# Stores and cache refills are issued from a lane that waits for the kernel's own count of engine time

## The chip, the cores and the metric

The kernel runs on one core of one Trainium2 chip. The metric is the device time of one execution in microseconds. A profile of one execution lists every instruction of the engines (TensorE = PE, VectorE = DVE, ScalarE = ACT, GpSimd = POOL) and the transfers that their queues issue; SyncE (SP) does nothing but issue transfers, in the order of its queue, and a transfer that must wait for its producer holds all that stands behind it.

## The reference

One layer of a hybrid encoder with D = 2048: 512 prompt tokens and 8 × 16 sample tokens, 640 columns together, float32.

```
z  = x @ w_in                     # all input projections in one
yA = (fox_attend(q, k, v, c) * silu(gate_a)) @ w_out_fox      # 8 heads of 128
       # logits + cumulative log forget gates, causal;
       # the sample tokens also see a cache of 512 keys and values per sequence
yB = (rms_norm(delta(q', k', v', g, beta)) * silu(gate_b)) @ w_out_gdn   # 8 heads of 128
       # q'|k'|v' = silu(depthwise conv of width 4); chunks of 64 tokens:
       # amat = I + strict_lower(kb @ k^T * decay)
       # u, w = triangular_solve(amat, v*beta), triangular_solve(amat, kb*exp(gc))
       # then a scan over chunks with a 128 x 128 state
h  = (sigmoid(m_a)*yA + sigmoid(m_b)*yB) @ w_out
x1 = LayerNorm(alpha*x + h)
y  = x1 + sigmoid(x1 @ w_pl_gate) * rms_norm(p @ w_pl_proj)
```

Outputs are y, the new keys, values and log forget values, the last convolution rows and the final DeltaNet states.

## The kernel before

**The stream.** Every large projection is cut into columns of 128 outputs; a column is a row of matmuls of 128x128 by 128x320 (two halves of the 640 tokens). For float32 accuracy each operand is split into a high and a low part (xh, xl, wh, wl), so that a product costs three matmuls. Some pairs of columns are done in a form with seven instead of eight block products; GpSimd forms the sums of their weights (ws, sb) ahead. Weights come by SyncE into tiles wr of 512 KB (three buffers, L269); ScalarE casts the high part (wh, L329) and VectorE subtracts it (wl, L335), or GpSimd fetches wl by a transfer that accumulates. These columns keep TensorE's queue filled.

**The steps between.** Attention and DeltaNet are Python generators, kept in lanes (`self.lane`). After every six matmuls of the stream the main program calls `tick()`. It looks at each lane in turn and, where the first generator of the lane is due, runs it to its next `yield`. `yield n` asks for n steps of pause; a negative n lets the next part start before the modelled end of the work just issued. The program is emitted under a manual schedule, so each engine's queue holds its instructions in the order in which these steps emit them.

**The planner.** While it emits, the kernel counts: `self.clock` is the modelled time of TensorE, advanced with each matmul, and `self.busy[e]` the modelled end of the last instruction of VectorE, ScalarE and GpSimd. A lane is due when its wake step and its modelled time have come.

**The stages that the change touches.** From about 730 to 960 us the stream carries the FoX heads (`phase_fox`). Per head: q, k, v are fetched from where they were stored; the bias rows nb and nbd are loaded (L637, L639); the prompt part goes through scores (L388), xs, pn; the sample part goes over the cached keys kc (`fox_dec`, scores at L773) and values vc (L813). When the scores over kc are done, the four kc loads for the next head are issued (`load_kv`, L627), and after the values the four vc loads. Each head's result og is stored to the scratch ogd (L830).

From about 960 to 1620 us the stream carries the DeltaNet heads (`phase_gdn`). A head's triangular matrix lt is inverted in blocks of 32 (`gdn_blocks`): four stores put the diagonal blocks to the scratch ld (L993), one load brings them back as lanes of 80 partitions (L998), and VectorE runs 31 pairs of a product and a subtraction on sx, which starts as the identity (L1004 and L1006). sx is stored (L1012), loaded again as u0 by `gdn_feed` (L1023), and `gdn_merge` puts the blocks of 32 together into uu: small matmuls on TensorE and copies on ScalarE and VectorE (L1060, L1068, L1072, L1074). uu is read by the head's scan over chunks (L1196, S at L1206). Beside that run the convolution of later channels (strip L865, cy L877 and L880, whose tail is stored at L884), the merge gates m (stored as md, L1572) and the FoX output projection fx (stored as fd, L1712).

The lanes are made in this order, in which each step visits them:

```
        self.outs, self.decs = self.lane(), self.lane()
        work, conv, self.ends = self.lane(), self.lane(True), self.lane()
        self.blocks, self.feeds, self.merge = self.lane(True), self.lane(True), self.lane()
        self.chunks, self.sums = self.lane(), self.lane(True)
```

## Time and profile before

| what | value |
|---|---|
| three runs | 2169.94, 2173.96, 2173.36 us; median 2173.36 |
| the profiled execution: its own time | 2173.18 us |
| its span in the profile | 2171.3 us |
| granted TensorE clock, mean | 0.999 |
| PE / DVE / ACT / POOL busy | 2149.0 / 1566.0 / 1007.3 / 401.9 us |
| bytes moved by DMA | 452.65 MB, mean 208 GB/s |

All rows come from that one execution. The page gives each engine's busy time and the groups of instructions by line; the windows give the same for a stretch of the span; the waits list says which instruction stood idle and whose end released it; the timeline lists single instructions by start, with the idle time before each in brackets. "SPq" is SyncE's queue: a wait there is time in which the transfer at its head could not be issued. Names as in `sx<-sx,lanes` are output and inputs. "L1004" is a line of the kernel before.

### The profile page before, as it was taken

The page shows a single profiled execution, that of the slowest core. Times are in us where ns is not written, and L with a number is a line of the kernel's source. Part 1 is how long each engine was busy: PE and PEld are TensorE (multiplying, and loading weights), DVE is VectorE, ACT ScalarE, POOL GpSimd, SP SyncE. Part 2 cuts the span into 40 slices and gives each one's busy share as a digit, 9 for nine tenths or more (in the row PEclk, how much of TensorE's full clock was granted, in tenths as well). Part 3 has the DMA queues.
Part 4 walks back from the last instruction along what each step waited for, and adds up shares of the span by engine and source line. Part 5 has one row for each costly group of instructions (what it writes and reads, how often), then busy time and mean ns, then how long its engine had stood idle before and what let it go on. Part 6 is the DMA issues. An engine that isn't in the chain of part 4 may idle for free.

```text
span 2171.3 us, 41951 instructions
## 1 busy us (share of the span) xinstructions
PE 2149.0 (99%) x15438; PEld 2082.3 (96%) x15438; DVE 1566.0 (72%) x3207; ACT 1007.3 (46%) x2213; POOL 401.9 (19%) x596
## 2 busy tenths in 40 slices
PE   9999999999999999999999999999999999999998
PEld 7799999999999998899999999999999999999998
DVE  5877776767776565566478677766757787789987
ACT  4344443443444343353655566655443343354544
POOL 0022233323330101002334333332000000021100
PEclk9999999999999999999999999999999999999999
DMA  6356656666554899869978778878567656673465
GB/s 235 101 184 202 189 182 199 198 199 194 184 180 158 276 325 344 314 199 291 241 179 199 180 188 194 189 182 248 161 229 260 209 171 202 201 276 122 153 227 173
DMA packets 240670, 452.65 MB, mean 208 GB/s; under 512 B 38920, under 2 KB 122504, under 8 KB 240464
## 3 DMA queue, kind: packets, MB, share of 16 engines
q1 hardware_dynamic: 224912, 421.64, 59.5%
q0 software_dynamic: 15552, 28.32, 8.0%
q8 instruction: 122, 2.00, 0.4%
q14 instruction: 84, 0.69, 0.1%
HBM read 353.48 MB, written 96.38 MB: 207 GB/s over the span
## 4 chain that ended last, share of the span: by engine, by line
PE 91%; DVE 3%; DMA 3%; ACT 1%; SPq 0%; issue 0%; POOL 0%; ACTq 0%; DVEq 0%; POOLq 0%
PE g L474 44%; PE g L396 18%; PE g L397 18%; PE g L440 2%; PE s L974 1%; PE s L742 1%; PE s L813 1%; PE s L773 1%; DMA ws138b<-ws 0%; PE s L440 0%; PE s L1168 0%; DMA nb<-rd 0%; DVE sx L1006 0%; DVE sx L1004 0%; PE s L726 0%
## 5 line engine op out<-in xcount | busy, mean ns | idle before, releaser
L329 ACT CAST wh<-wr 128x512 fp32r<-128x512 f32 x624 | 381.2, 619 | 288.7 <-PE g L474 109.5
L335 DVE TENSOR_TENSOR wl<-wr,wh 128x512 fp32r<-128x512 f32 x516 | 358.3, 708 | 183.5 <-ACT wh L329 173.7
L474 PE MATMUL g<-xh,wh 128*128 128x320 f32 (+1 forms) x1296 | 402.9, 311 | 2.7 <-ACT m L1278 1.6
L474 PE MATMUL g<-xl,wh 128*128 128x320 f32 (+1 forms) x1296 | 401.2, 310 | 0.6 <-DVE xl L371 0.6
L474 PE MATMUL g<-xh,wl 128*128 128x320 f32 (+1 forms) x1296 | 401.4, 310 | 0.0
L396 PE MATMUL g<-xh,wh 128*128 128x320 f32 (+1 forms) x960 | 313.0, 326 | 0.7 <-ACT wh L329 0.7
L396 PE MATMUL g<-xh,wl 128*128 128x320 f32 (+1 forms) x960 | 297.1, 309 | 0.8 <-DMA wl<-in_w 0.7
L396 PE MATMUL g<-xl,wh 128*128 128x320 f32 (+1 forms) x960 | 297.2, 310 | 0.4 <-DVE xl L371 0.4
L397 PE MATMUL g<-xh,wh 128*128 128x320 f32 x960 | 297.3, 310 | 0.0
L397 PE MATMUL g<-xl,wh 128*128 128x320 f32 x960 | 297.0, 309 | 0.0
L397 PE MATMUL g<-xh,wl 128*128 128x320 f32 x960 | 296.7, 309 | 0.0
L474 PEld LDWEIGHTS g<-xh,wh 128*128 128x128 f32 x1296 | 243.9, 188 | 4.3 <-ACT m L1278 2.1
L474 PEld LDWEIGHTS g<-xl,wh 128*128 128x128 f32 x1296 | 243.7, 188 | 1.1 <-DVE xl L371 1.1
L474 PEld LDWEIGHTS g<-xh,wl 128*128 128x128 f32 x1296 | 244.1, 188 | 0.0
L474 PE MATMUL g<-t,wh 128*128 128x320 f32 (+1 forms) x1088 | 241.4, 310 | 0.0
L335 DVE TENSOR_TENSOR wl<-sr,wh 128x512 fp32r<-128x512 f32 x200 | 147.9, 759 | 98.6 <-ACT wh L329 97.6
L295 POOL TENSOR_TENSOR ws<-ws 128x171 f32<-128x171 f32 (+2 forms) x152 | 116.7, 768 | 541.5 <-DMA ws<-in_w 535.7
L396 PEld LDWEIGHTS g<-xh,wh 128*128 128x128 f32 x960 | 180.9, 188 | 11.9 <-issue 7.1
L474 PEld LDWEIGHTS g<-t,wh 128*128 128x128 f32 x1088 | 181.9, 188 | 0.6 <-issue 0.3
L396 PEld LDWEIGHTS g<-xh,wl 128*128 128x128 f32 x960 | 180.6, 188 | 1.4 <-DMA wl<-in_w 1.0
L397 PEld LDWEIGHTS g<-xh,wh 128*128 128x128 f32 x960 | 181.0, 189 | 0.9
L396 PEld LDWEIGHTS g<-xl,wh 128*128 128x128 f32 x960 | 180.9, 188 | 1.0 <-DVE xl L371 1.0
(440 smaller groups left out, 4148.8 us busy)
## 6 DMA issues: line engine op xcount, KB each, us to landing
wr<-in_w SPq DMA_DIRECT2D x252, 512.0 KB
wl<-in_w POOLq DMA_DIRECT2D x108, 256.0 KB, 5.8
kc<-in_kc SPq DMA_DIRECT2D x32, 512.0 KB
vc<-in_vc SPq DMA_DIRECT2D x32, 512.0 KB
sr<-in_w SPq DMA_DIRECT2D x25, 512.0 KB
ws<-in_w SPq DMA_DIRECT2D x96, 128.0 KB
sb<-in_w SPq DMA_DIRECT2D x80, 128.0 KB
md<-m SPq DMA_DIRECT2D x32, 320.0 KB
```

The source lines that it names most:

```text
L295: nc.gpsimd.tensor_tensor(out=o, in0=x, in1=y, op=op)
L329: nc.scalar.copy(out=hi, in_=src)
L335: nc.vector.tensor_tensor(out=lo, in0=src, in1=hi.bitcast(F32), op=ALU.subtract)
L396: nc.tensor.matmul(ps[0], whl[w], xhl[o][:, a], start=(first and x == 0), stop=(last and x == 2))
L397: nc.tensor.matmul(ps[1], whl[w], xhl[o][:, b], start=(first and x == 0), stop=(last and x == 2))
L440: nc.tensor.matmul(ps, x[:, sl], w, start=(s == 0 and n == 0), stop=(s == 15 and n == 2))
L474: nc.tensor.matmul(ps, a[:, w], b, start=(k == 0 and n == 0 and not more), stop=(k == last and n == 2), skip_group_check=True)
L742: nc.tensor.matmul(ops[:, 0:P], vn[:, kb, :], pT[:, kb * P:(kb + 1) * P], start=(kb == 0), stop=(kb == i))
L773: nc.tensor.matmul(s1[32 * j:32 * j + 32, :], self.qpad[:, 2 * j + par, :], kc[:, (j % 2) * NPT:(j % 2 + 1) * NPT], start=(par == 0), stop ...
L813: nc.tensor.matmul(od[32 * j:32 * j + 32, 0:P], self.ppad[:, c, 2 * j + par, :], vc[:, o:o + P], start=False, stop=(par == 1 and c == 3), ...
L974: nc.tensor.matmul(pp[:, o:o + 256].rearrange("p (a b) -> p a b", a=2), kq[:, 0, x], kq[:, :, x], start=True, stop=True)
```

## The change

A new lane `puts` is visited first at every step. `put` (a store) and `call` (any issue) append to it a generator that lets steps pass until `self.clock` has reached a given time, issues, and ends; the lane is first in, first out, and issues at most one entry per step. Without a time given, the time is the modelled end of the busiest of the three engines at the moment of the call, plus 0.5 us.

Through it now go the FoX store of og, the refills of kc and vc (at the step's own time plus 0.5 us), the store of the convolution's tail, and the stores md and fd. The stage's end also waits for the lane to be empty. In the DeltaNet stage, `gdn_blocks` fetches the identity first, then waits for the modelled end of VectorE's work plus 0.25 us before it issues the four ld stores; the lanes load stands five steps after these, as before. `gdn_feed` pauses 3 and 5 steps where it paused 5 and 7, and the stores of sx, og and st of the DeltaNet heads stand one step later.

```
+    def put(self, out, in_, t=None):
+        self.call(lambda: self.nc.sync.dma_start(out=out, in_=in_), t)
+    def call(self, fn, t=None):
+        t = max(self.busy) + 0.5 if t is None else t
+        def wait():
+            while self.clock < t:
+                yield 1
+            fn()
+            yield
+        self.puts["gens"].append(wait())
...
@@ fox_dec: after the scores over kc, and likewise "v" after the values
-            for j in range(4):
-                self.load_kv(h + 1, "k", j)
+            self.call(lambda: [self.load_kv(h + 1, "k", j) for j in range(4)], self.clock + 0.5)
...
@@ fox_out
-        nc.sync.dma_start(out=self.ogd[h], in_=og)
+        self.put(out=self.ogd[h], in_=og)
...
@@ likewise put(...) for o["conv"][:, ct, :] <- tail, md[nm] <- m, fd[nf] <- t
...
@@ gdn_blocks (ready = self.busy[0] + 0.25 when the head's lt is done)
+        x = self.zt([80, 8, 32], "sx")
+        nc.sync.dma_start(out=x.rearrange("p c i -> p (c i)"), in_=self.i["eye"])
+        while self.clock < ready:
+            yield 1
         for a in range(4):
             sl = slice(32 * a, 32 * a + 32)
             nc.sync.dma_start(out=self.ld[:, a].rearrange("t j i -> j t i"), in_=lt[sl, :, sl])
         yield 5
-        x = self.zt([80, 8, 32], "sx")
-        nc.sync.dma_start(out=x.rearrange("p c i -> p (c i)"), in_=self.i["eye"])
         lanes = self.zt([80, 32, 32], "lanes")
...
+        yield 1
         self.inv = h
...
@@ gdn_feed
-        yield 5
+        yield 3
...
-        yield 7
+        yield 5
...
@@ gdn_out, ahead of the store of og, and gdn_dec, ahead of the store of st
+            yield 1
...
@@ run
+        self.puts = self.lane(True)
         self.outs, self.decs = self.lane(), self.lane()
...
@@ phase_gdn, end
-        self.until(lambda: self.gdone == 7 and not self.sums["gens"])
+        self.until(lambda: self.gdone == 7 and not self.sums["gens"] and not self.puts["gens"])
```

Fifty stores and sixteen refills of four loads go through the lane. TensorE's instructions are the same in number and kind. Three places show how the queues differ.

VectorE in the DeltaNet stage, where head 5's merge (uu) meets the solve of head 6 (sx, lanes). Before:

```order
L1060 TENSOR_SCALAR uu_11303<-s 32x4x32 x2
L1004 TENSOR_TENSOR sx_17586<-sx,lanes 80x8x31
L1006 TENSOR_TENSOR sx<-sx,sx_17586 80x8x31
...
L1004 TENSOR_TENSOR sx_17586<-sx,lanes 80x8x22
L1006 TENSOR_TENSOR sx<-sx,sx_17586 80x8x22
L1074 TENSOR_SCALAR uu_11303<-s 64x4x64
```

In the new program (L1076, L1090, L1019 and L1021 are the old L1060, L1074, L1004 and L1006; the rest of the output norm of an earlier head stands in the lines left out):

```order
L1076 TENSOR_SCALAR uu_11303<-s 32x4x32 x2
L873 MEMSET strip 128x3
L878 COPY strip<-cvst 128x8x3
L893 SCALAR_TENSOR_TENSOR cy<-strip,taps,cy 128x664 x3
...
L1125 TENSOR_TENSOR rfy<-rfy,cs 128x5
L1090 TENSOR_SCALAR uu_11303<-s 64x4x64
L1019 TENSOR_TENSOR sx_17676<-sx,lanes 80x8x31
L1021 TENSOR_TENSOR sx<-sx,sx_17676 80x8x31
```

Ten pairs of the solve stood between the two instructions on uu; now the solve begins behind the second.

SyncE in the FoX stage, between head 4 and head 5 (ogd is head 4's result, kc the refill for head 5, nb and nbd the bias rows of head 5). Before:

```order
L269 DMA wr<-in_w 128x1024
L830 DMA ogd_72<-og 128x640
L627 DMA kc<-in_kc 128x1024 x4
L637 DMA nb<-rd 128x640
L639 DMA nbd<-sfd 128x1x512
L291 DMA ws<-in_w 128x256 x4
L269 DMA wr<-in_w 128x1024
```

In the new program (L151 is `put`):

```order
L284 DMA wr<-in_w 128x1024
L652 DMA nb<-rd 128x640
L654 DMA nbd<-sfd 128x1x512
L151 DMA ogd_72<-og 128x640
L642 DMA kc<-in_kc 128x1024 x4
L306 DMA ws<-in_w 128x256 x4
L284 DMA wr<-in_w 128x1024
```

The two bias loads now stand ahead of the store and the refill.

SyncE around the solve of head 6. Before:

```order
L993 DMA ld<-lt 32x5x32 x4
...
L269 DMA wr<-in_w 128x1024
L291 DMA ws<-in_w 128x171 x4
L996 DMA sx<-in_eye 80x256
L998 DMA lanes<-ld 80x1x1024
```

In the new program:

```order
L306 DMA ws<-in_w 128x171 x4
L1005 DMA sx<-in_eye 80x256
L1010 DMA ld<-lt 32x5x32 x4
L284 DMA wr<-in_w 128x1024
L1235 DMA out_stp<-S 128x128
L1114 DMA og<-sgf_181 128x640
L1013 DMA lanes<-ld 80x1x1024
```

The identity stands ahead of the ld stores; a weight load, a state store and a gate load stand between these and the lanes load.

## The prediction, on record before the changed kernel ran

> **What bounds the kernel now.** I read the engine totals first, then the busy time by stage, then who waits for whom, then the two places where TensorE stood still for a reason that the change touches.

> ```profile
> span 2171.3 us, 41951 instructions
> PE 2149.0 (99%) x15438; PEld 2082.3 (96%) x15438; DVE 1566.0 (72%) x3207; ACT 1007.3 (46%) x2213; POOL 401.9 (19%) x596
> ```

> TensorE is busy 2149.0 of 2171.3 us: 22.3 us are not matmul, whatever the other engines do. The windows below have, after the window and its length, the busy time of PE, PEld, DVE, ACT and POOL, then clock, DMA share and GB/s.

> ```profile
> core 0: us, PE busy (x) PEld busy (x) DVE busy (x) ACT busy (x) POOL busy (x), PEclk, DMA share, GB/s
> 730.00:960.00 230.00, 227.01 (x2020) 208.53 (x2019) 140.54 (x328) 95.83 (x245) 16.81 (x32) 1.00 0.87 307
> 1040.00:1440.00 400.00, 398.14 (x3053) 381.47 (x3051) 284.25 (x934) 243.83 (x677) 146.80 (x250) 1.00 0.83 193
> 1440.00:1620.00 180.00, 176.79 (x1354) 168.98 (x1355) 122.23 (x351) 85.77 (x228) 23.19 (x42) 0.99 0.69 206
> ```

> The change touches the FoX stage (first row) and the DeltaNet stage (the others). TensorE idles there 2.99 + 1.86 + 3.21 = 8.06 us: length less busy time, row by row. That is 0.37% of the kernel and all that better order can give; 0.2% (4.35 us), about what a measurement of this kernel can tell from no change, is over half of it. Who keeps TensorE waiting, FoX first, then DeltaNet (total, times, longest):

> ```profile
> PE s L754 <- ACT pn L801: 0.8, 1, 0.8
> PE s L388 <- ACT pn L801: 0.8, 1, 0.8
> PE s L388 <- DVE xd L780: 0.7, 2, 0.5
> ...
> PE s L1196 <- DVE uu L1074: 1.9, 1, 1.9
> PE s L1072 <- issue: 0.9, 2, 0.7
> PE s L1168 <- DVE S L1206: 0.9, 1, 0.9
> PE g L396 <- DMA wl<-in_w: 0.7, 1, 0.7
> ```

> Only the last names a transfer. SyncE's queue shows much more waiting:

> ```profile
> SPq L269 <- DVE wl L335: 424.0, 152, 9.0
> SPq L1012 <- DVE sx L1006: 41.5, 6, 9.1
> SPq L1712 <- ACT fx L1711: 28.8, 8, 7.8
> SPq L1572 <- ACT m L1571: 24.2, 9, 6.4
> SPq L627 <- PE s L813: 17.3, 6, 5.7
> SPq L830 <- DVE og L829: 10.6, 5, 2.9
> ```

> The change addresses all but the first row, 122.4 us of a queue that a store or refill holds until its producer is done. Yet 424.0 us of the same queue are weight loads (L269) waiting for a buffer that VectorE has still to read. A load released earlier would wait there instead.

> **The change part by part.** The numbers of matmuls, casts and bytes stay; what changes is when a transfer enters SyncE's queue, and in the DeltaNet stage when VectorE's solve enters its own.

> *Stores put off (ogd, convolution tail, md, fd).* Fifty stores leave at a later step, when the kernel's own count says the producer is done. What is queued behind them, weight loads above all, moves up. Saving on TensorE: 0, because none of its waits above is for a weight load of SyncE (`wl<-in_w` is issued by GpSimd), and the cover is the buffers loaded ahead: 424.0 us of waiting for them to be emptied. Were that cover gone, the longest hold, 7.8 us, would be the price once; nothing points to it. Against it, the source tile comes free later by a step or two. One step is six matmuls of the stream, seen below as the distance between two equal ones, 0.87 us. A tile late by two steps costs at most 1.74 us; I take 0, since no wait of TensorE here has a store behind it.

> *kc and vc refills put off.* Head 5's refill in the trace, with what it held up:

> ```profile
> 846.87 3.20 SPq L627 DMA_DIRECT2D kc<-in_kc  x4
> 850.12 0.42 SPq L637 DMA_DIRECT2D nb<-rd  x1
> ...
> 859.36 0.35 DVE L759 SCALAR_TENSOR_TENSOR xs<-nb,colT,s 128x128 f32<-128x128 f32 x1 [2.76 <-DMA nb<-rd]
> 868.67 0.34 DVE L780 SCALAR_TENSOR_TENSOR xd<-nb,colT,s 128x128 f32<-128x128 f32 x1
> ...
> 865.26 1.92 PE L773 MATMUL s<-kc,qpad 128*32 128x512 f32 x16
> 869.06 0.44 PE L388 MATMUL s<-kh,qh 128*128 128x384 f32 x1 [0.45 <-DVE xd L780]
> ```

> The bias row nb goes out behind four refill loads of 512 KB, VectorE waits 2.76 us for it, and ten microseconds later TensorE waits 0.45 us for VectorE. In the new order nb, nbd and the ogd store stand ahead of the refill, so nb leaves about 3.2 us sooner. I take −0.45 (ends: 0, if VectorE catches up its own delay elsewhere, and −0.45). The refill itself leaves about two steps later, 1.74 us and the three transfers' issue, at nb's 0.42 us each, some 3 us. It is needed at 865.26, 18.4 us after its old issue; 2.1 MB at the stage's 307 GB/s is 6.8 us, an estimate from the windows row. Some 8 us stay spare: 0.

> *The block solve of DeltaNet.* The identity load moves ahead of the four ld stores, the lanes load follows them by five steps as before, the solve (sx) follows the lanes load by five steps as before, and some later steps move by one or two either way. It matters because VectorE's queue is in order. Head 6 in the trace:

> ```profile
> 1430.23 0.78 SPq L998 DMA_DIRECT2D lanes<-ld  x1
> 1431.22 0.58 DVE L1060 TENSOR_SCALAR uu<-s 32x128 f32<-32x128 f32 x2
> 1437.38 0.41 DVE L1004 TENSOR_TENSOR sx<-sx,lanes 80x248 f32<-80x248 f32 x1 [5.58 <-DMA lanes<-ld]
> 1439.05 0.17 DVE L865 COPY strip<-cvst 128x24 f32<-128x24 f32 x1
> 1439.31 0.85 ACT L877 ACTIVATE cy<-strip,taps 128x664 f32<-128x664 f32 x1 [4.52 <-DVE strip L865]
> 1440.19 0.37 ACT L1068 COPY t<-s 64x256 f32<-64x256 f32 x1
> 1440.65 0.65 PE L1072 MATMUL s<-uu,t 64*64 64x64 f32 x8 [0.70 <-issue]
> 1447.01 0.42 DVE L1074 TENSOR_SCALAR uu<-s 64x256 f32<-64x256 f32 x1
> 1447.48 0.49 PE L1196 MATMUL s<-vr,uu 128*128 128x128 f32 x2 [1.92 <-DVE uu L1074]
> ...
> 1438.77 0.31 PE L397 MATMUL g<-xh,wl 128*128 128x320 f32 x1
> 1439.64 0.31 PE L397 MATMUL g<-xh,wl 128*128 128x320 f32 x1
> ```

> The lanes load takes 7.15 us from issue (1430.23) to VectorE's start (1437.38). Five steps are 4.35 us, so VectorE blocks 5.58 us on head 6's first sx. Behind it stand the strip copy, for which ScalarE waits 4.52 us, then ScalarE's copy t and TensorE's L1072, 0.70 us late; and after ten sx pairs head 5's uu, for which TensorE waits 1.92 us. In the new order head 6's solve begins after that uu. Both waits go: −2.62 (ends: 0, if what then precedes uu is as late, and −2.62).

> The five steps from lanes to sx stay, so a lanes load can be late again, in front of something else. Before, it was late four times:

> ```profile
> DVE sx L1004 <- DMA lanes<-ld: 11.4, 4, 5.6
> ```

> 11.4 us of blocked VectorE cost TensorE 2.62 once: 0.65 for each late load. The steps of the new order put the short distances at heads 0, 1, 4 and 7. Of these, heads 0 and 7 have no uu or S behind sx that is nearly due, head 4 little, and head 1 stands ahead of head 0's merge. I charge one mean price, +0.65 (ends: 0, and two full collisions, +5.24).

> [...]

> *Extra steps* (xd, ogd, sts stores one later; the feed four shorter). Counted in steps, heads 3 and 6 start their solve eight later, and the last head is done three or four later, some 3 us. None of TensorE's waits is for u0, og or st, and the cover is the matmul stream, which goes on to 1620 and beyond: 0, with one step, 0.87, to either side.

> Sum, against the profiled execution's own 2173.18 us: −0.45 − 2.62 + 0.65 = −2.42, which gives 2170.8. That execution lies 0.18 below the median of the runs, 2173.36.

> **The rivals.** *Queue time turns into TensorE time (faster).* For it: over 120 us of held queue, and a DMA share of 0.87 and 0.83 in which earlier loads could spread. With half of the remaining 4.99 us (8.06 − 3.07) gone as well: 2173.18 − 3.07 − 2.50 = 2167.6; all gone: 2165.1. Against it: the two pn waits are turnarounds TensorE–ScalarE–TensorE with no transfer in them, and S is an in-order pile on VectorE.

> *Late lanes before a due uu or S (slower).* Each such collision costs 2.62. With two on top of both gains: 2173.18 − 3.07 + 5.24 = 2175.4; with three: 2178.0. It decides from the third on, since 2177.7 is 0.2% above the median. For it: no step was added between lanes and sx, while og loads and a state store now go in between, and the four late loads before show that the distance is too short. Against it: three of the four before cost nothing.

> *Only the queue changes (no effect).* Both gains are there by chance order, and new waits as small take their place: 2173.2. [...]

> **How the numbers follow.** Four cases. The forecast, one or both gains and at most one small new wait, 2168.5 to 2172.5: 0.46. Only the queue changes, 2172.5 to 2174, with a tail for a transfer come late, kc above all: 0.20. Queue time turned into TensorE time, 2165.1 to 2169.0: 0.20. Two or more collisions, from 2174 up: 0.14. Faster by 0.2% means under 2169.0: the third case and 0.04 of the forecast's lower edge, 0.24. Slower means over 2177.7: half of the fourth case, 0.07, and the second's tail, 0.05, together 0.12. The rest, 0.64, is no change. For eight in ten the range goes from 2166.5, most of the waits gone, to 2176.5, two collisions and 1 us of scatter; outside lie 0.07 below and 0.13 above.

> **What would show it.** After the change TensorE's wait for uu at L1196 (now another line) and the L1072 stop are gone, and head 6's first sx comes behind head 5's uu. VectorE's wait for nb near 859 shrinks to under 1 us. SyncE's waits for fx, m, og and sx fall from over 100 us to under 30, and the waits of weight loads for wl grow by as much. VectorE's waits for lanes stay near 11 us. TensorE's idle time over the three windows falls from 8.06 to about 5.6 us. I am wrong if TensorE waits on S, uu or t1 behind a blocked sx more than once, if it waits for kc at L773, or if a weight load appears among its releasers.

## The result, and the profile after

The changed kernel takes 2186.33 us (median of five runs, 2184.78 to 2195.00) against 2173.36 us: slower, by a ratio of 1.0069 with a 95% interval of 1.0052 to 1.0086. The forecast was 2170.8 us with a range from 2166.5 to 2176.5. The profiled execution took 2184.78 us, with a span of 2182.8 us. Ratios here and below are those of fast runs: one execution of 3492 us and one of 7296 us, of two kernels further below, are not in them. The page's first lines, and then the three windows of the stages that the change touches (columns as in the prediction):

```profile
span 2182.8 us, 41942 instructions
PE 2153.7 (99%) x15438; PEld 2086.8 (96%) x15438; DVE 1568.3 (72%) x3207; ACT 1008.8 (46%) x2213; POOL 408.1 (19%) x596
```

```profile
730.00:960.00 230.00, 225.33 (x2000) 207.08 (x1999) 138.89 (x325) 94.09 (x241) 15.99 (x30) 0.99 0.86 304
1040.00:1440.00 400.00, 393.28 (x2983) 377.31 (x2982) 280.37 (x908) 240.62 (x662) 146.41 (x243) 0.99 0.82 189
1440.00:1620.00 180.00, 176.81 (x1380) 168.12 (x1379) 122.53 (x357) 87.22 (x234) 25.71 (x49) 0.99 0.66 194
```

The matmuls are the same 15438, yet PE is busy 4.7 us longer, and its idle time in the three windows rose from 8.06 to 4.67 + 6.72 + 3.19 = 14.58 us, where 5.6 was forecast. Both grew, and the busy part is not work: the granted clock is 0.99 where it was 1.00. The waits of TensorE after the change, FoX (its one new row) and then DeltaNet:

```profile
PE g L412 <- ACT e L1806: 2.3, 1, 2.3
...
PE s L1082 <- DVE t L1068: 3.0, 1, 3.0
PE s L1175 <- DVE og L1134: 2.3, 1, 2.3
PE s L1157 <- DMA st<-in_st: 2.3, 1, 2.3
PE s L1157 <- POOL ws L310: 0.9, 1, 0.9
PE s L1206 <- DVE S L1222: 0.8, 1, 0.8
PE s L1059 <- DVE m L1051: 0.6, 1, 0.6
```

The wait for uu and the stop at L1072 are gone, as forecast. Four stops of 2.25 to 2.96 us are new (a stop is a time in which TensorE stands still). Behind each of them the granted clock falls to 0.50, called half clock below. These windows, cut at the clock's own steps, show it (the eighth value is PEclk; the last row, of the kernel before, is the one such period that it had, behind its stop for uu):

```profile
942.46:945.87 3.41, 3.41 (x13) 3.41 (x14) 2.23 (x5) 2.33 (x5) 0.00 (x0) 0.50 0.27 104
1147.26:1150.67 3.41, 3.41 (x14) 3.32 (x14) 3.26 (x8) 2.76 (x8) 0.66 (x1) 0.50 0.70 167
1410.08:1413.49 3.41, 3.41 (x26) 3.03 (x16) 3.21 (x10) 0.27 (x1) 0.00 (x0) 0.50 0.84 275
1522.72:1526.13 3.41, 3.25 (x24) 2.89 (x25) 3.31 (x8) 1.49 (x3) 0.00 (x0) 0.50 0.90 353
...
1448.03:1451.44 3.41, 3.41 (x15) 3.41 (x14) 3.31 (x10) 2.16 (x4) 0.61 (x1) 0.50 1.09 290
```

Each is 3.41 us long at 0.50, so each loses 1.71 us: four against one is 5.1 us more, which the busy time shows as its 4.7.

Matching the stream's matmuls of the two traces one by one shows where the difference arose. The shift is how much later (+) or sooner (−) the same matmul starts in the changed kernel; a row has what the shift grew by at that place:

| place in the kernel before | shift of the stream | what it is |
|---|---|---|
| up to 730 us | −0.8 | a wait for wh at 361 us that came out shorter; nothing there was changed |
| FoX, 730 to 921 | −0.8 | the bias row nb in time |
| around 942 | +3.6 | one md store |
| around 1043 | −1.0 | a weight load, wl, in time |
| DeltaNet, 1043 to 1615 | +9.0 | the stops for t, og and st, less the one for uu |
| around 1625 | +1.8 | fx and weights of the last columns |
| sum | +11.8 | |

**The md store.** SyncE, ScalarE and TensorE at the end of FoX, the kernel before and then the changed one:

```profile
934.90 0.33 SPq L1572 DMA_DIRECT2D md<-m  x1
937.89 0.74 ACT L1793 ACTIVATE eacc<-e 128x640 f32<-128x640 f32 x1 [0.47 <-DVE e L1788]
```

```profile
932.50 0.77 ACT L1590 ACTIVATE m<-g 128x320 f32<-128x320 f32 x2 [0.90 <-PE g L411]
936.26 0.33 SPq L1808 DMA_DIRECT2D ed<-e  x1
936.64 0.42 SPq L151 DMA_DIRECT2D md<-m  x1
941.27 0.74 ACT L1812 ACTIVATE eacc<-e 128x640 f32<-128x640 f32 x1 [5.47 <-DMA md<-m]
942.38 0.59 PE L412 MATMUL g<-ph,wh 128*128 128x320 f32 x1 [2.25 <-ACT e L1806]
```

m is done at 933.27. Put off, its store falls behind the store of e, which waits for e, and leaves at 936.64, 3.4 us after m; in the kernel before it left as soon as m was done, at 934.90. But the tile of m is the next one to be written, as eacc. ScalarE waits 5.47 us for the store to land, the copy that frees TensorE's accumulator waits behind that, and TensorE stands still for 2.25 us.

**The solve of head 1.** VectorE in the kernel before, then SyncE, VectorE and TensorE in the changed one, by engine (L1052 and L1068 are the same line):

```profile
1129.92 0.41 DVE L1004 TENSOR_TENSOR sx<-sx,lanes 80x248 f32<-80x248 f32 x1 [1.57 <-DMA lanes<-ld]
1135.29 0.28 DVE L1052 TENSOR_SCALAR t<-s 32x128 f32<-32x128 f32 x1
```

```profile
1115.87 0.34 SPq L1028 DMA_DIRECT2D xd<-sx  x1
1121.00 0.33 SPq L1005 DMA_DIRECT2D sx<-in_eye  x1
...
1121.91 0.42 SPq L919 DMA_DIRECT2D gr<-rd  x1
...
1131.72 0.80 SPq L1013 DMA_DIRECT2D lanes<-ld  x1
...
1127.26 1.40 DVE L953 SCALAR_TENSOR_TENSOR dt<-gr,colT,cb 128x128 f32<-128x128 f32 x5 [10.69 <-DMA gr<-rd]
1136.33 0.42 DVE L1019 TENSOR_TENSOR sx<-sx,lanes 80x248 f32<-80x248 f32 x1 [4.91 <-DMA lanes<-ld]
1146.01 0.28 DVE L1068 TENSOR_SCALAR t<-s 32x128 f32<-32x128 f32 x1
...
1131.57 0.44 PE L1059 MATMUL s<-m,lt 32*32 32x32 f32 x16 [0.63 <-DVE m L1051]
1146.44 0.65 PE L1082 MATMUL s<-t,lt 64*64 64x64 f32 x8 [2.96 <-DVE t L1068]
```

The identity goes into the tile sx, from which head 0's result is still being stored (1115.87): it waits 4.7 us for that store to land and holds SyncE's queue, and with it gr, the ld stores, u and the lanes load. VectorE idles 10.69 us for gr; that is not all loss, since in the kernel before it idled 8.76 us at the same place for u. Then the lanes of head 1 come 4.91 us late, in front of head 0's t. The lateness is not the whole of it: in the new order eight pairs of the solve, a strip copy and a norm stand between the late lanes and t, 9.7 us from the first sx to t, where six pairs, 5.4 us, stood before.

**og and st.** No late lanes stand before the stop for og. VectorE has no idle time from 1389.5 us on, and og, at 1408.91, comes behind the solve's pairs, a norm, and a step of the convolution. The stop for st is one for a transfer: the state load leaves at 1516.02, behind loads of ogr in SyncE's queue that wait up to 5.1 us, and TensorE has nothing left to do at 1520.6.

SyncE's queue changed for the most part as the change says:

```profile
SPq L284 <- DVE wl L350: 441.6, 152, 9.0
SPq L284 <- ACT wl L347: 150.1, 34, 9.8
SPq L642 <- PE s L827: 17.9, 7, 5.5
SPq L151 <- ACT fx L1730: 14.2, 5, 6.7
SPq L1028 <- DVE sx L1021: 10.6, 5, 3.6
SPq L1005 <- DMA xd<-sx: 9.0, 3, 4.7
SPq L151 <- ACT m L1590: 6.5, 2, 4.3
```

The waits for sx, fx and m fell from 94.5 to 31.3 us, the weight loads wait 17.6 us longer for VectorE's wl and 31.1 us longer for ScalarE's (119.0 before), and the identity's 9.0 us are new. The refills hold the queue for TensorE as long as before (17.9 and 17.3 us).

### The profile page after: what moved, and what is told of

The parts are those of the page before. It is cut to its first block, busy times and chain, and to the rows that moved or that the text cites. A ratio compares the mean times of both kernels' runs of the same rounds, so it can differ in the third digit from the quotient of the medians.

```text
span 2182.8 us, 41942 instructions
## 1 busy us (share of the span) xinstructions
PE 2153.7 (99%) x15438; PEld 2086.8 (96%) x15438; DVE 1568.3 (72%) x3207; ACT 1008.8 (46%) x2213; POOL 408.1 (19%) x596
## 4 chain that ended last, share of the span: by engine, by line
PE 91%; DMA 3%; DVE 3%; ACT 1%; issue 1%; SPq 1%; POOL 0%; ACTq 0%; DVEq 0%; POOLq 0%
PE g L489 43%; PE g L411 19%; PE g L412 18%; PE g L455 2%; PE s L987 1%; DMA wr<-in_w 1%; PE s L757 1%; PE s L827 1%; PE s L788 1%; PE s L1185 0%; PE s L455 0%; PE s L741 0%; ACT wh L344 0%; DVE sx L1021 0%; DVE sx L1019 0%
## 5 line engine op out<-in xcount | busy, mean ns | idle before, releaser
L489 PEld LDWEIGHTS g<-xl,wh 128*128 128x128 f32 x1296 | 243.6, 188 | 1.1 <-DVE xl L386 1.1
L489 PEld LDWEIGHTS g<-xh,wl 128*128 128x128 f32 x1296 | 244.1, 188 | 0.0
L411 PEld LDWEIGHTS g<-xl,wh 128*128 128x128 f32 x960 | 181.7, 189 | 1.1 <-DVE xl L386 1.1
L412 PEld LDWEIGHTS g<-xl,wh 128*128 128x128 f32 x960 | 181.3, 189 | 0.0
```

Source lines behind the costliest of these rows:

```text
L411: nc.tensor.matmul(ps[0], whl[w], xhl[o][:, a], start=(first and x == 0), stop=(last and x == 2))
L412: nc.tensor.matmul(ps[1], whl[w], xhl[o][:, b], start=(first and x == 0), stop=(last and x == 2))
L489: nc.tensor.matmul(ps, a[:, w], b, start=(k == 0 and n == 0 and not more), stop=(k == last and n == 2), skip_group_check=True)
```

## Experiments

A ratio is to the kernel before, run beside it on the same chip. The stream's shift is that of the profiled execution against that of the kernel before, near 2030 us, worked out as in the table.

### Which part loses

**The lane alone**: the DeltaNet functions as before, the order on VectorE that of before.

```
 # changed kernel
-    gdn_blocks: identity first, wait for ready
-    gdn_feed: yield 3 / yield 5;  yield 1 ahead of the stores of sx, og, st
+    gdn_blocks, gdn_feed, gdn_out, gdn_dec of the kernel before
```

> The store lane and the refills of the change, with the block solve of DeltaNet (identity, pauses, extra steps) as before: VectorE's order is that of before. Theory (the DeltaNet loss comes from the changed order of the solve on VectorE, the FoX loss from one md store put off): the trace of the changed kernel loses 2.25 us at 942 behind that store and 1.71 us to the half clock after it, and gains about 0.7 in FoX, so 2173.4 + 3.96 - 0.7 = 2176.7, and 2178.5 if the stop of 1.7 us at 1632 (fx) is made by the lane too; TensorE stops at uu as before (1.9 us near 1447). Rival (the lane's reordering of SyncE's queue causes the DeltaNet stops): 2183 or more, with stops at 1146, 1410 and 1522.

Measured: 2175.57 us, ratio 1.0007 (0.9997 to 1.0017), shift +3.0 us. The DeltaNet waits are those of before:

```profile
PE s L1209 <- DVE uu L1087: 1.9, 1, 1.9
PE s L1085 <- issue: 1.0, 2, 0.8
```

Reordering fifty stores and fourteen refills (keys and values of seven heads; the first head's loads do not go through the lane) moved the DeltaNet stage by −1.0 us (from +2.27 at 1019 to +1.26 at 1615). At 942 it lost 2.1 us, in stops of 0.9 and 0.6 us for e among others, with no half clock behind them.

**The DeltaNet edits alone**: all stores and refills issued at once.

```
-    self.put(out=..., in_=...)                 # 4 places
+    nc.sync.dma_start(out=..., in_=...)
-    self.call(lambda: [self.load_kv(...) ...], self.clock + 0.5)
+    for j in range(4): self.load_kv(...)
```

> The DeltaNet edits alone, all stores and refills issued at once as before: VectorE's order is that of the changed kernel. Theory: no stop at 942, the stops of the DeltaNet stage stay; 2186.3 - 4.0 + 0.7 = 2183 (2181 if the stop at 1632 goes as well). Rival (the lane causes the DeltaNet stops): 2171 to 2176.

Measured: 2182.21 us, ratio 1.0042 (1.0031 to 1.0054), shift +7.1. The waits of TensorE between 1040 and 1620:

```profile
PE s L1084 <- DVE t L1070: 3.2, 1, 3.2
PE s L1177 <- DVE og L1136: 2.3, 1, 2.3
PE s L1159 <- POOL ws L310: 0.9, 1, 0.9
PE s L1208 <- DVE S L1224: 0.8, 1, 0.8
```

t, og, ws and S are those of the changed kernel; they come with the DeltaNet edits. The wait for st (2.25 us at 1523) is missing: it needs both parts. The shifts of the parts, 3.0 and 7.1, fall 1.7 us short of the whole, 11.8; here the stop for t drew two periods of half clock, which makes up for some of the missing stop.

### The two single places

**One store of fifty issued at once.**

```
-        self.put(out=self.md[self.nm], in_=m)
+        if tag == "eacc":
+            nc.sync.dma_start(out=self.md[self.nm], in_=m)
+        else:
+            self.put(out=self.md[self.nm], in_=m)
```

> The changed kernel, with one store of 50 taken out of the lane: the md store whose tile is used again as eacc at the end of FoX. Theory: ScalarE's wait of 5.5 us for that store goes, with it TensorE's stop of 2.25 us and the half clock after it (1.71 us): 2186.3 - 4.0 = 2182.3. Rival (the squares of e are late for another reason): 2186.

Measured: 2183.15 us, ratio 1.0042 (1.0027 to 1.0058). The store leaves at 932.46 and eacc waits 0.47 us as before; the stop at 942 and its half clock are gone, which shows the cause. The median fell by 3.2 us where 4.0 was expected. In the two profiles the stream gains the whole 4.0 us at 942; part of it is lost again at 1141, where the stop for t is 3.4 us long and is followed by two periods of half clock instead of one.

**The identity fetched with the lanes again.**

```
 gdn_blocks
-        x = ...; dma_start(x <- eye)      # ahead of the wait and the ld stores
         while self.clock < ready: yield 1
         ... ld stores; yield 5
+        x = ...; dma_start(x <- eye)
         lanes = ...
```

> The changed kernel with the identity fetched just ahead of the lanes load, as before, instead of ahead of the ld stores; VectorE's order is that of the changed kernel. Theory (the identity waits for the store of the head before, 9.0 us in three waits, and holds ld, the next head's gr and u behind it, so that lanes come late): SyncE's three waits go, lanes of head 1 land 3 to 4.7 us sooner, and of the stops at 1131 to 1147 (0.63 + 2.96 + 1.71 for the clock = 5.3 us) most go: 2181 to 2183. Rival (the distance from lanes to the solve in steps decides, wherever the identity stands): 2186, stop at 1146 unchanged.

Measured: 2182.15 us, ratio 1.0036 (1.0023 to 1.0048): 4.2 us less. VectorE's order is the changed kernel's, and the stream's shift differs from it at one place, by 3.6 us at head 1's solve:

```profile
1117.93 0.46 SPq L919 DMA_DIRECT2D gr<-rd  x1
1129.14 0.80 SPq L1013 DMA_DIRECT2D lanes<-ld  x1
...
1134.18 0.41 DVE L1019 TENSOR_TENSOR sx<-sx,lanes 80x248 f32<-80x248 f32 x1 [5.34 <-DMA lanes<-ld]
1144.26 0.65 PE L1082 MATMUL s<-t,lt 64*64 64x64 f32 x8 [1.59 <-DVE t L1068]
```

SyncE's three waits for the identity are gone. gr leaves 4.0 us sooner and lanes 2.6, so that the solve starts 2.2 us sooner and the stop for t is 1.59 instead of 2.96 us, with no half clock behind it. The time came as expected, but the lanes were to land 3 to 4.7 us sooner, and for VectorE they are as late as ever (5.34 us). Of the 5.3 us lost at head 1 (0.63 + 2.96 + 1.71) the identity's move made 3.6; in what stays, t stands behind the same eight pairs and norm.

**Both.** The two edits above together.

> The changed kernel with both single repairs: the one md store issued at once, and the identity fetched with the lanes. Theory (the two losses are separate places): they add, 2186.3 - 3.5 - 4.2 = 2178 to 2179; the stops at 1410 and 1520 stay. Rival (one repair moves the loss to the other place): 2182.

Measured: 2178.36 us, ratio 1.0027 (1.0015 to 1.0039). They add, as expected. The stops for og (2.31 us) and st (1.5 us) stay; in the profiled execution, the fastest of its kernel with 2174.33 us, neither is followed by half clock.

### The distance and the pauses

**Nine steps from lanes to the solve**, in the changed kernel and in the kernel before:

```
-        yield 5
+        yield 9
         tmp = self.zt([80, 8, 32], "sx2")
```

> The changed kernel with nine steps instead of five between the lanes load and the solve. Theory (late lanes block VectorE ahead of head 0's t): VectorE's waits for lanes, 13.5 us, fall under 2, the stop at 1146 (2.96 + 1.71) goes, 2181.6, unless the later solve collides elsewhere. Rival (the stop is a pile of VectorE work whatever the lanes do): 2186.

> The kernel before with nine steps instead of five between the lanes load and the solve, nothing else. Theory: VectorE's waits for lanes, 11.4 us, fall under 2, the stops at 1440 and 1447 (0.70 + 1.92) and the half clock after them (1.71) go: 2173.4 - 4.3 = 2169.1, if the later solve meets nothing due. Rival (any shift of the solve costs, as the changed kernel's did): 2176 or more, with stops for t, S or og behind sx.

Measured: 2180.75 us (ratio 1.0042, 1.0027 to 1.0057) and 2177.87 us (1.0031, 1.0022 to 1.0041). In the changed kernel the stop for t falls from 2.96 to 0.6 us, as expected, but not because its lanes come in time. The one late load that is left is head 1's, in front of this t, and later than in the changed kernel:

```profile
1138.99 0.41 DVE L1019 TENSOR_TENSOR sx<-sx,lanes 80x248 f32<-80x248 f32 x1 [8.91 <-DMA lanes<-ld]
```

Four pairs and the norm now stand between it and t, not eight, so that t comes 0.57 us sooner; and TensorE asks for t twelve matmuls of the stream later, which is two steps or 1.74 us. Together that is the 2.3 us by which the stop shrank. In the kernel before, waits for lanes fall to 0.5 us in all; there the stops at 1440 and 1447 are gone, and at 1615 its stream was 10 us ahead, in part because the last head's small matmuls were still to come. Then both lose it, and the second more than it had won:

```profile
1638.95 1.35 PE L1117 MATMUL s<-cb,ob 128*128 128x128 f32 x4 [5.40 <-ACT ob L1112]
```

Eight heads, each four steps later, end with a last head for whose output the stream has to stop 5.4 us, with two periods of half clock. So a longer distance takes these stops away, but the theory that the lanes' lateness makes them is not shown: in the changed kernel the order decided, and in the kernel before lateness and order changed together. Waiting longer everywhere is no cure: of the second kernel's expectations the rival's number came true, for a reason of its own.

**The pauses of the solve's tail as before**, the rest of the change kept.

```
 gdn_feed
-        yield 3   ...   yield 5
+        yield 5   ...   yield 7
 gdn_blocks, gdn_out, gdn_dec
-        yield 1          # ahead of the stores of sx, og, st
```

> The changed kernel with the pauses of the solve's tail as before (feed 5 and 7 instead of 3 and 5, no extra step ahead of the stores of sx, og and st); identity ahead, wait for VectorE's count and store lane remain. Theory (each shift of the DeltaNet steps against the stream moves VectorE's pile in front of something due; the tail pauses make the stops at 1396 to 1410, 0.8 + 2.3 + 1.7, and 1523, 2.3 + 1.7): these go, the stop at 1146 behind head 1's solve stays: 2186.3 - 8.8 = 2177.5, with 2 to 4 us back if the new order makes a stop of its own. Rival (the wait for VectorE's count, which shifts heads 3 and 6, makes them): 2184 to 2188.

Measured: 2185.69 us, ratio 1.0066 (1.0051 to 1.0081). The stops for og and st are gone, as the theory said, with the wait for VectorE's count still there, which speaks against the rival's mechanism. But they are gone as well with nine steps from lanes to the solve, where the pauses of the changed kernel stay; so it is not the pauses alone that make them. Yet the number is the rival's: TensorE now stops 5.3 us for t at 1142, because head 1's lanes come 9.2 us late. The expectation allowed 2 to 4 us for a new collision; it cost all that was won.

### What a stop costs

**Eleven stops put into the kernel before**, of different lengths.

```
+        # every 25 steps from step 1690
+        p = self.sps(); nc.tensor.transpose(p[:, 0:P], self.ident, self.ident)
+        nc.vector.tensor_copy(out=z, in_=p[0:80, 0:P])
+        for _ in range(n - 1): nc.vector.tensor_single_scalar(z, z, 1.0, op=ALU.mult)
+        nc.tensor.matmul(p[:, 0:P], z, self.ident[0:80, :], start=True, stop=True)
```

> The kernel before with eleven stops of TensorE put into the stream between about 1640 and 1870 us, 22 us apart: a transpose, a chain of 1 to 15 VectorE operations on it, and a matmul that waits for the chain; the results are not used. Theory (a stop of TensorE longer than some 1.7 to 1.9 us is followed by 3.41 us at half clock, 1.71 us lost, a shorter one by nothing): the clock record shows 0.5 after each of the long stops and after none of the short ones, whatever the order of their lengths. Rival (the half clock comes at moments that don't depend on the stop's length): no such border.

Measured, the ten stops that the trace lists and the half clock at each (VectorE's own work lengthened some chains; the run's mean granted clock is 0.991):

| stop, us | 0.38 | 2.00 | 2.18 | 2.32 | 2.58 | 2.65 | 3.23 | 5.67 | 5.72 | 6.16 |
|---|---|---|---|---|---|---|---|---|---|---|
| at half clock, us | 0 | 3.41 | 0 | 3.41 | 0 | 3.41 | 6.83 | 6.83 | 6.83 | 6.83 |

The border that I expected does not exist: a stop of 2.00 us is punished and one of 2.58 is not. In these traces the half clock starts at multiples of 3.413 us from one another: here at 1796.66, 1847.86 and 1905.88, which lie 15 and 17 times 3.413 us apart, in the changed kernel at 942.46, 1147.26, 1410.08 and 1522.72, which lie 60, 77 and 33 times apart. So I cut the trace at that grid and call one of its periods a cell. Around the stops of 2.00 and 2.58 us:

```profile
1793.25:1796.66 3.41, 1.41 (x10) 1.19 (x9) 3.10 (x8) 0.64 (x2) 0.00 (x0) 1.00 0.56 190
1796.66:1800.07 3.41, 3.41 (x15) 3.41 (x14) 0.69 (x1) 0.62 (x1) 0.00 (x0) 0.50 0.34 123
...
1817.14:1820.55 3.41, 2.52 (x18) 2.24 (x16) 3.21 (x8) 1.23 (x3) 0.00 (x0) 1.00 0.96 295
1820.55:1823.97 3.42, 1.73 (x12) 1.73 (x13) 1.43 (x7) 0.47 (x1) 0.00 (x0) 1.00 0.48 170
1823.97:1827.38 3.41, 3.41 (x25) 3.41 (x24) 1.87 (x3) 1.13 (x3) 0.00 (x0) 1.00 0.40 135
```

The first stop falls into one cell of the grid, leaves TensorE 1.41 us of work in it, and the next cell runs at half clock. The second is longer and lies across two cells, with 2.52 and 1.73 us of work: no half clock. The idle share is 0.59 in the cell of the first, and 0.26 and 0.49 in the two of the second.

### A version that is faster by 0.1%

**Head 6's solve alone put off**, in the kernel before, and the same with the lane and the md repair; and the lane with the md repair by itself.

```
-        yield 5
+        yield 11 if h == 6 else 5
         tmp = self.zt([80, 8, 32], "sx2")
```

> The kernel before with eleven steps instead of five between the lanes load and the solve for head 6 alone: head 5's uu then stands behind two pairs of the solve, not ten, and no lanes load is late there. Theory: the stops at 1440 and 1447 (0.70 + 1.92) and the half clock after them (1.71) go, nothing else moves: 2172.5 - 4.3 = 2168 to 2169. Rival (the delayed solve stands in front of og, S or dt of the neighbours and makes a stop of its own): 2171 to 2176.

> The store lane and refills of the change without the DeltaNet edits, the one md store (tile eacc) issued at once, and the delay of head 6's solve. Theory: the gains of the lane in FoX (nb, 0.7) and at 1043 (wl, 1.0) come on top of head 6's 4.3: 2172.5 - 6.0 = 2166.5. Rival (the lane's gains are no more than the scatter): as the same without the lane.

> The store lane and refills of the change without the DeltaNet edits, and with the one md store (tile eacc) issued at once. Theory: the 2.1 us that the lane alone lost at 942 go; left are its gains, 0.7 in FoX and 1.0 at 1043, less some 1.7 at 1625 where ob waited: 2172 to 2173, no difference from before. Rival (the lane itself is worth something beyond these places): 2170 or less.

Measured: 2169.61, 2168.44 and 2172.32 us, with ratios of 0.9990 (0.9981 to 0.9999), 0.9990 (0.9981 to 0.9999) and 1.0001 (0.9992 to 1.0010). Moving the one solve that stood in front of a due uu takes the stops at 1440 and 1447 away, and is worth about 2 us, half of what I expected, and just clear of the noise. In the trace of the first another place, near 1285, took a half clock that it had not had before: matmuls of 0.47 us from 1286.17 on, of 0.31 us ahead of it. Nor was the half clock behind uu always there to be won: in the trace of the third the same stop for uu is 1.9 us long, and the granted clock from 1440 to 1620 us is 1.00, where the kernel before has 0.99. The lane, repaired, is worth nothing that can be measured: the ratio of 0.9990 is the same with it and without it.

## Why the prediction was wrong, point by point

**Head 6 (−2.62).** Right, and in these two profiles too small: the waits for uu and at L1072 went, and so did the half clock behind them, 1.71 us, which not every execution has. The clock of 0.99 stood in the prediction's own row for 1440 to 1620; I read that row for its idle time alone.

**nb (−0.45).** Right: VectorE's wait for nb is gone, TensorE's wait for xd is down to 0.3 us in one place, and the stream gains 0.8 us there.

**Stores put off (0).** This step failed. I looked for waits that stores had caused and found none, and bounded a tile that comes free later by two steps, 1.74 us. A store put off does not fall two steps back but behind whatever then stands in the queue, here a store of e that waited for its own producer: it left 3.4 us after m was done. The tile was the very next to be written: a stop of 2.25 us, and 1.71 for the clock. Taking this one store out of the lane gave 3.2 us back.

**The identity (no term).** This step failed as well. I counted its move ahead of the ld stores as a reordering; it is a transfer into a tile that a store is still reading, so it brings a wait into SyncE's queue (9.0 us in three), and gr and lanes stood behind it. Putting it back gave 4.2 us.

**Late lanes (+0.65).** The mechanism was named, at the right head (head 1 ahead of head 0's merge), and VectorE's waits for lanes stayed near what was forecast (13.5 us against 11.4). The price failed: the mean over four late loads says nothing of the one that has a due instruction behind it. That one cost 0.63 + 2.96 + 1.71 = 5.3 us, of which the identity made 3.6, and order had its part beside lateness. Head 1's lanes load took 4.6 us from issue to VectorE's start (1131.72 to 1136.33). The slower rival came nearest the time, and in part by luck: I had asked for three collisions of 2.62 us behind late lanes; of t, og and st only t stood behind late lanes, and with the half clock one stop was worth up to twice the price.

**Extra steps (0 within ±0.87).** Failed: I took 0 because no wait of TensorE was for u0, og or st, but the change of the steps made waits where there were none. The stops for og (2.3 us) and st (2.25 us), each with 1.71 us of half clock, went when the pauses were put back, though the collision at t then grew by as much. They also went with nine steps from lanes to the solve; what in the new order makes them is not shown.

**Queue time.** The forecast that freed queue time turns into longer waits of weight loads held: 63 us less for sx, fx and m, 48.7 us more for wl of VectorE and ScalarE together. The lane with its one fault repaired is 1.0001 of the kernel before: a new order within the queue was worth nothing where no tile was due. The md store (2.25 us, and 1.71 for the clock) and the identity (9.0 us of waits in SyncE's queue) show the exception: there the order decided who waited for whom.

Of the signs that were to show the prediction wrong, none came as written: TensorE waited once behind a blocked sx, and neither kc nor a weight load is among its releasers. Waits for a store that frees a tile (eacc), for og and for a state load were not on the list.

Not settled is why S, t and og pile up so differently with each shift; each of five shifts of the solve that were tried made stops of its own, in places that I could not name ahead.

## What to carry to other kernels

Before putting a store off, look up who writes its tile next, and before fetching ahead, look up what still reads the tile: here both turned a transfer off the path into a wait in SyncE's queue, of 3.4 us for the md store and of 9.0 us in three for the identity. This kernel, whose main engine is 99% busy, had nothing to win from freeing a queue that this engine hardly waited for (1.0001), but four stops of 2.25 to 2.96 us on that engine cost another 1.71 us each. Where steps of two pipelines are interleaved by hand, move the one step that collides; the general shifts tried here traded their stops for others.

## What the runs showed of the hardware

| trace | cell starts at, us | TensorE busy, us | idle share | clock of the next cell |
|---|---|---|---|---|
| before | 96.35 | 1.78 | 0.48 | 1.00 |
| before | 1444.61 | 1.50 | 0.56 | 0.50 |
| changed | 95.95 | 2.39 | 0.30 | 1.00 |
| changed | 1519.31 | 1.32 | 0.61 | 0.50 |
| changed | 939.04 | 1.17 | 0.66 | 0.50 |
| changed | 1406.67 | 1.11 | 0.67 | 0.50 |
| changed | 1143.84 | 0.82 | 0.76 | 0.50 |
| eleven stops | 1817.14 | 2.52 | 0.26 | 1.00 |
| eleven stops | 1960.50 | 2.02 | 0.41 | 1.00 |
| eleven stops | 1820.55 | 1.73 | 0.49 | 1.00 |
| eleven stops | 1793.25 | 1.41 | 0.59 | 0.50 |
| eleven stops | 1844.45 | 1.09 | 0.68 | 0.50 |
| eleven stops | 1902.47 | 1.09 | 0.68 | 0.50 |

In these cells a share up to 0.49 was followed by full clock and one from 0.56 on by half.

There is an exception: in the kernel before with head 6's solve put off, the half clock follows the cell at 1282.66, which has a stop of only 0.86 us, 2.55 us of work and an idle share of 0.25. In the kernel before, the cell at 1280.77 has the same stop and the same 2.55 us of work, and full clock follows. What makes the difference is not shown.

Stops of 1.92 to 2.96 us were thus enough when they fell wholly or mostly into one cell, and those of 2.18 and 2.58 us that lay across two cells drew none. The same stop did not always cost the same: behind the one for uu the kernel before lost 1.71 us (1.92 us long, in one cell), and the lane with the md repair none (1.9 us long, granted clock 1.00 from 1440 to 1620 us).
